# Last group's sums stored by POOL's own queue, and the weight rows for the sums loaded from the fifth step on

## The chip, the core and the metric

The kernel runs on one core of a Trainium2 chip. TensorE (PE) multiplies, VectorE (DVE), ScalarE (ACT) and GpSimd (POOL) work element by element, and SyncE (SP) issues most of the transfers between the chip's main memory and the on-chip buffer. Each engine works its own list of instructions in the order in which they stand; an instruction that waits holds up all behind it on that engine or queue. The metric is the time of the whole program on the device, in microseconds: 1392.29 us before, the median of 3 runs (1391.9 to 1397.92).

## The reference

One encoder layer on 1024 tokens of width 1024: a mixer (mLSTM and neighbourhood attention), then an MLP, then a gated embedding. The change lies in the MLP's second half:

```
z = einsum('bsd,df->bsf', rms_norm(h, norm2_g), w_ff1)        # 1024 x 4096
h = h + einsum('bsf,fd->bsd', square(relu(z)), w_ff2)         # back to 1024 x 1024
gate = sigmoid(einsum('bsd,de->bse', rms_norm(h, ple_norm_g), w_ple_gate))
h = h + gate * einsum('bsk,kd->bsd', p, w_ple_up)
```

## The kernel before

Everything is computed transposed (features on partitions, tokens along the free axis). Every float32 operand of a product is split into a rounded high half and a low half, `hi` by ACT and `lo = raw - hi` by DVE, and each product is three passes on PE: hi x hi, hi x lo, lo x hi (`passes`). Big products are done by Strassen-Winograd: both operands are cut into 2 x 2 blocks, and seven products of sums of blocks replace eight.

**First half of the MLP (`ff1`).** A loop over 16 groups c of 256 of the 4096 inner features. `products` makes a group's blocks in `z{c}_0` and `z{c}_1`; `finish(c)` (L1286) scales and clips them on DVE (L1290), squares them on ACT (L1291), and makes the sums of blocks that Winograd needs next, four POOL operations: `t3`, `t2` into the tile `tz` (L1302, L1303), then two in place in the z tiles (L1306, L1308). All blocks and sums are stored to the scratch tensors `zd[0]` to `zd[3]` in main memory: `put` (L1296) sends three through ACT's queue and the four that POOL made through `PQ`, which is SP's queue.

**Second half (`ff2`).** Four sweeps, `ff2_sweep` (L1377), in the order 2, 0, 1, 3. A sweep walks the 16 groups in steps c = 0 to 15 and adds 24 matmuls a step into eight PSUM banks (L1390, tile `f_P`). A step needs its two operands, each in halves: from `zd[i]` the tile `zr` is loaded (L1276) and split into `zh` (ACT, L1277) and `zl` (DVE, L1278); from w_ff2 the tile `w2r` is loaded in two pieces (L1235) and split into `w_Nh` (ACT, L138) and `w_Nl` (DVE, L141; N is the step). The operands of steps 0, 1 and 2 of the first sweep are asked for while the last group of the first half is still worked on (`ff2_early`); those of the later steps follow by `step(i, c)`. `zr`, `zh`, `zl`, `w_Nh` and `w_Nl` have two buffers each, `w2r` has three: so `w2r` of step c+3 is loaded when `w_Nl` of step c is done, and `w_Nh` of step c+2 can be made when PE has done step c.

**The sums of weight rows.** Sweeps 0 and 1 need Winograd sums of blocks of w_ff2. `w2_load(c)` loads two full row blocks, `w2re` (even) and `w2ro` (odd), 512 KB each; `w2_sums(c)` makes four DVE operations of 128 x 512 of them (L1250 to L1253). `w2re` has six buffers, `w2ro` two, so the third `w2ro` waits for the first pair's sums. During the first sweep the table `ahead` tells after which step which load or sum is asked for; five pairs are summed there, the rest in sweep 0.

The program's text sets which buffers and dependencies there are; a scheduler then puts the instructions in order on every engine and queue, so a moved line shifts its neighbours too. Each transfer that SP or ACT issues takes one of eight completion counters in turn and waits until the transfer eight before it has landed.

Of the kernel before, what the change touches and what calls it, by code (L numbers as in the profile page):

```python
# [59 lines left out]
def tile_block(ctx, tc, xT, pT, w_in, w_out, w_ff1, w_ff2, w_gate, w_up, vecs, gate_b, rpbp, con,  # L60
               outT, dbg=None):
    nc = tc.nc
# [18 lines left out]
    def utile32(name):  # L81
        return big.tile([P, T], F32, tag="u", bufs=16, name=name)
# [33 lines left out]
    zd = [dr.tile([P, FF // 256, T], F32, name=f"zd{i}") for i in range(3)]  # L116
# [1066 lines left out]
    NC_ = FF // 256  # L1183
# [6 lines left out]
    with tc.tile_pool(name="ff1", bufs=1) as ff1:  # L1190
# [37 lines left out]
        PQ = nc.sync  # L1228
# [57 lines left out]
        def finish(c):  # L1286

            z = zt.pop(c)
            for z_ in z:
                V.scalar_tensor_tensor(z_, z_, 0.0, Rb, op0=ALU.max, op1=ALU.mult)  # L1290
                S.activation(z_, z_, AF.Square)  # L1291
            b11, b12, b21, b22 = z[0][:, 0:512], z[0][:, 512:], z[1][:, 0:512], z[1][:, 512:]
            tz = utile32(f"tz{c}")
            t3, t2 = tz[:, 0:512], tz[:, 512:]

            def put(i, s, src):  # L1296
                (PQ if (i, s) in ((0, 1), (1, 1), (1, 0), (3, 0)) else nc.scalar).dma_start(zd[i][:, c, s * 512 : (s + 1) * 512], src)

            put(2, 1, b11)
            put(2, 0, b21)  # L1300
            put(0, 0, b22)
            G.tensor_tensor(t3, b22, b12, op=ALU.subtract)  # L1302
            G.tensor_tensor(t2, t3, b11, op=ALU.add)  # L1303
            put(0, 1, t2)
            put(1, 1, t3)
            G.tensor_tensor(b12, b12, b11, op=ALU.subtract)  # L1306
            put(1, 0, b12)
            G.tensor_tensor(b21, b21, t2, op=ALU.subtract)  # L1308
            put(3, 0, b21)
# [49 lines left out]
    with tc.tile_pool(name="ff2", bufs=2) as ff2:  # L1359
# [108 lines left out]
            E_.tensor_tensor(hres[e][:, cs], hres[e][:, cs], z, op=ALU.add)  # L1468
            nc.sync.dma_start(outT[e * P : (e + 1) * P, cs], hres[e][:, cs])

        ahead = {4 + 2 * c: [(w2_sums, c), (w2_load, c + 2)][: 2 if c < 4 else 1] for c in range(5)}
        ahead[2] = [(w2_load, 0), (w2_load, 1)]
        op, _ = ff2_sweep(2, 0, ("P2", "P1"), pre, ahead, 0)
        op, _ = ff2_sweep(0, 1, ("P3", "P6"), op, {}, 1)
        early3, u_tile = [], utile
# [114 lines left out]
```

## Time and profile before

| what | us |
|---|---|
| median of 3 runs | 1392.29 |
| the profiled execution's own time | 1395.88 |
| its span, first to last instruction | 1394.1 |
| PE busy | 1320.1 (95%) |
| DVE busy | 904.5 (65%) |
| ACT busy | 590.4 (42%) |
| POOL busy | 491.2 (35%) |

The first half of the MLP ends at about 982 us of the span; the first sweep of the second half runs to about 1079 us, the last to about 1299 us, the gate to the end. Shares of the whole span tell little here: PE is nearly always busy, and what counts is where it is not. A step of a sweep is 24 matmuls; a wait of PE at a step shows in the list of waits as PE at `f_P L1390` waiting for a half `w_Nh` or `w_Nl` of that step. The mean granted clock of TensorE over the span is 0.964.

### The profile page before, as it was taken

To read this page: it belongs to the slowest core of one execution; us is meant where nothing else is said; L and a number is where in the kernel's file an instruction comes from. 1 tells how busy PE (TensorE), PEld (TensorE's weight loads), DVE (VectorE), ACT (ScalarE), POOL (GpSimd) and SP (SyncE) were. 2 spreads that over 40 slices of the span, in tenths; PEclk is the share of its full clock that TensorE was granted. 3 is DMA by queue.
4 is the path that set the end of the run, shared out by engine and by line. 5 is a ranking of instruction groups with operands and counts; after the bars stand their busy time and mean duration, and the time that the engine had idled before them with its cause. 6 is when DMAs were issued, how large, how long until landed. Compare 5 with 4: busy or idle time off the path is not lost.

```text
span 1394.1 us, 19257 instructions
## 1 busy us (share of the span) xinstructions
PE 1320.1 (95%) x7115; PEld 1106.7 (79%) x7115; DVE 904.5 (65%) x1435; ACT 590.4 (42%) x955; POOL 491.2 (35%) x392
## 2 busy tenths in 40 slices
PE   7999999999998899997899999999799999999998
PEld 5988778799897677775678888888588888888887
DVE  4486786665672555669856666666565987559543
ACT  7353434264553545545333333333333434545321
POOL 2215675463331111106355556665300000007422
PEclk9999999999998798998899999999899999999999
DMA  8553333475322553311154444554787863542342
GB/s 295 195 151 90 112 111 107 150 249 167 112 62 98 167 168 135 112 46 45 31 166 145 149 136 151 166 166 144 255 307 242 263 199 99 171 145 70 106 143 83
DMA packets 153422, 206.03 MB, mean 148 GB/s; under 512 B 17776, under 2 KB 102768, under 8 KB 153328
## 3 DMA queue, kind: packets, MB, share of 16 engines
q1 hardware_dynamic: 144656, 185.77, 41.6%
q10 hardware_dynamic: 7200, 13.11, 2.8%
q0 software_dynamic: 1472, 5.92, 1.2%
q8 instruction: 56, 0.92, 0.3%
q14 instruction: 38, 0.31, 0.1%
HBM read 151.60 MB, written 53.17 MB: 147 GB/s over the span
## 4 chain that ended last, share of the span: by engine, by line
PE 61%; DMA 5%; DVE 4%; issue 2%; ACT 1%; POOL 1%; SPq 0%; DVEq 0%; ACTq 0%; POOLq 0%
PE f_P L1390 21%; PE p_s_t L256 9%; PE g L1459 6%; PE p L256 6%; PE op L1023 4%; PE p_s L256 3%; PE p_t L256 3%; DMA tab<-tabI 2%; PE pv L995 1%; PE pt L975 1%; PE o1p L310 1%; DMA nr<-qnd 1%; DVE h L1025 1%; DMA wo_0r<-w_out 1%; PE sc L945 1%
## 5 line engine op out<-in xcount | busy, mean ns | idle before, releaser
L1413 POOL TENSOR_TENSOR h<-h,evP 128x512 f32<-128x512 f32 x8 | 14.8, 1886 | 249.2 <-ACT evP L1404 249.2
L256 PE MATMUL p<-b,w_ah 128*128 128x512 f32 x256 | 80.4, 396 | 3.4 <-DVE b L193 3.4
L1278 DVE TENSOR_TENSOR zl<-zr,zh 128x1024 fp32r<-128x1024 f32 x56 | 69.1, 1237 | 11.0 <-ACT zh L1277 11.0
L964 POOL TENSOR_SCALAR pc<-pc,st 128x288 f32<-128x288 f32 (+1 forms) x32 | 17.5, 546 | 159.1 <-DVE st L959 128.9
L1277 ACT ACTIVATE zh<-zr 128x1024 fp32r<-128x1024 f32 x56 | 58.5, 1049 | 23.7 <-DMA zr<-zd 12.2
L260 DVE TENSOR_TENSOR z<-z,p_s_t 128x512 f32<-128x512 f32 x64 | 42.5, 685 | 33.4 <-PE p_s_t L256 32.1
L256 PEld LDWEIGHTS p<-b,w_ah 128*128 128x128 f32 x256 | 49.0, 192 | 14.1 <-DVE b L193 3.9
L954 ACT ACTIVATE pc<-pc,st 128x288 f32<-128x288 f32 (+1 forms) x64 | 36.3, 568 | 53.6 <-DVE st L953 53.5
L256 PE MATMUL p<-b,w_al 128*128 128x512 f32 x128 | 50.9, 399 | 7.7 <-DVE w_al L141 7.7
L1302 POOL TENSOR_TENSOR tz<-z,z 128x512 f32<-128x512 f32 x16 | 26.2, 1639 | 81.0 <-ACT z L1291 81.0
L953 DVE CUSTOM_DVE_ANT_1 pc<-sc,tab 128x288 f32<-128x288 f32 (+1 forms) x64 | 29.8, 503 | 38.2 <-DMA tab<-tabU 16.8
L1459 PE MATMUL g<-gh,wg_h 128*128 128x512 f32 (+1 forms) x136 | 51.6, 380 | 0.0
L1459 PE MATMUL g<-gh,wg_l 128*128 128x512 f32 (+1 forms) x136 | 51.3, 377 | 0.0
L1459 PE MATMUL g<-gl,wg_h 128*128 128x512 f32 (+1 forms) x136 | 51.2, 377 | 0.0
L788 POOL TENSOR_SCALAR wv<-vh,wj 128x129 f32<-128x129 f32 x56 | 30.7, 551 | 57.4 <-PE num L789 52.8
L1290 DVE SCALAR_TENSOR_TENSOR z<-z,Rb 128x1024 f32<-128x1024 f32 x32 | 50.2, 1573 | 0.9 <-ACT Rb L180 0.9
L138 ACT ACTIVATE w_bh<-w_0r 128x1024 fp32r<-128x1024 f32 x16 | 17.0, 1061 | 73.0 <-POOL w_0r L234 53.3
L138 ACT ACTIVATE w_ah<-w_0r 128x1024 fp32r<-128x1024 f32 x16 | 17.0, 1062 | 68.4 <-PE p_t L256 68.4
L256 PE MATMUL p_s_t<-bt,w_bh 128*128 128x512 f32 x128 | 41.9, 410 | 3.4 <-ACT w_bh L138 3.4
L1291 ACT ACTIVATE z<-z 128x1024 f32<-128x1024 f32 x32 | 33.9, 1060 | 22.1 <-DVE z L1290 21.8
L141 DVE TENSOR_TENSOR w_cl<-w_1r,w_ch 128x1024 fp32r<-128x1024 f32 x16 | 23.1, 1443 | 29.2 <-ACT w_ch L138 29.0
L256 PE MATMUL p_s<-b,w_bh 128*128 128x512 f32 x128 | 40.0, 394 | 0.0
(719 smaller groups left out, 4602.5 us busy)
## 6 DMA issues: line engine op xcount, KB each, us to landing
zr<-zd SPq DMA_DIRECT2D x56, 512.0 KB
zd<-z ACTq DMA_DIRECT2D x48, 256.0 KB
w2r<-w_ff SPq DMA_DIRECT2D x48, 256.0 KB
w_0r<-w_ff SPq DMA_DIRECT2D x16, 512.0 KB
w_1r<-w_ff SPq DMA_DIRECT2D x16, 512.0 KB
zd<-tz SPq DMA_DIRECT2D x32, 256.0 KB
zd<-z SPq DMA_DIRECT2D x32, 256.0 KB
w2re<-w_ff SPq DMA_DIRECT2D x16, 512.0 KB
```

Of the source, the lines that this page charges most:

```text
L138: mark["hi"] = S.activation(hi, raw, AF.Copy).ins
L256: TE.matmul(ps, x_, y_, start=j == 0 and i == 0, stop=j == 3 and i == 2)
L260: mark["add"] = V.tensor_tensor(o, a, b, op=ALU.add).ins
L788: G.tensor_scalar(wv, vh[:, c, 0:129], wj[:, col], 1.0, op0=ALU.mult, op1=ALU.mult)
L954: S.activation(pb, pb, AF.Exp, scale=-1.0, bias=st[:, 0:1], accum_out=st[:, 1:2])
L1023: TE.matmul(ps, a, b, start=n == 0 and i == 0, stop=n == len(ks) - 1 and i == 2)
L1277: S.activation(hi, raw, AF.Copy)
L1278: dv.append(V.tensor_tensor(lo, raw, hi.bitcast(F32), op=ALU.subtract).ins)
L1290: V.scalar_tensor_tensor(z_, z_, 0.0, Rb, op0=ALU.max, op1=ALU.mult)
L1291: S.activation(z_, z_, AF.Square)
L1390: pe_last = TE.matmul(ps[n, e], a, b, start=st and k == 0, stop=sp and k == 2)
L1459: TE.matmul(ps, x_, y_, start=k == 0 and i == 0, stop=k == KT - 1 and i == 2)
```

## The change

`finish` of the last group (c = 15) sends the four stores of POOL's sums through POOL's own queue; those of the other 15 groups stay on SP's. The table `ahead` loads the first two pairs after step 5 instead of after step 2, and asks for the sums, each with the load of a later pair, after steps 6, 8, 10, 12, 14 instead of 4, 6, 8, 10, 12.

```diff
             def put(i, s, src):
-                (PQ if (i, s) in ((0, 1), (1, 1), (1, 0), (3, 0)) else nc.scalar).dma_start(zd[i][:, c, s * 512 : (s + 1) * 512], src)
+                ((nc.gpsimd if c == NC_ - 1 else PQ) if (i, s) in ((0, 1), (1, 1), (1, 0), (3, 0)) else nc.scalar).dma_start(zd[i][:, c, s * 512 : (s + 1) * 512], src)
...
-        ahead = {4 + 2 * c: [(w2_sums, c), (w2_load, c + 2)][: 2 if c < 4 else 1] for c in range(5)}
-        ahead[2] = [(w2_load, 0), (w2_load, 1)]
+        ahead = {6 + 2 * c: [(w2_sums, c), (w2_load, c + 2)][: 2 if c < 4 else 1] for c in range(5)}
+        ahead[5] = [(w2_load, 0), (w2_load, 1)]
```

SP's queue before, from the load of `zr` for step 2 of the first sweep on (in these names `zr2_3` is sweep 2, step 3; `w2re_0` is the even row block of pair 0; a last number is the buffer's; `zd1`, `zd0`, `zd3` are the scratch tensors that the sums of group 15 go to):

```order
L1276 DMA zr2_2_9101<-zd2_108 128x1024
L1235 DMA w2ro_0_9216<-w_ff2 128x1024
L1235 DMA w2re_1_9218<-w_ff2 128x1024
L1235 DMA w2ro_1_9220<-w_ff2 128x1024
L1276 DMA zr2_3_9222<-zd2_108 128x1024
L1297 DMA zd1_107<-tz15_9118 128x512
L1297 DMA zd0_106<-tz15_9118 128x512
L1297 DMA zd1_107<-z15_0_8974 128x512
L1235 DMA w2r2_3_9228<-w_ff2 128x512
L1297 DMA zd3_109<-z15_1_8975 128x512
L1235 DMA w2r2_3_9228<-w_ff2 128x512
```

SP's queue now, at the same place:

```order
L1276 DMA zr2_3_9214<-zd2_108 128x1024
L1276 DMA zr2_2_9101<-zd2_108 128x1024
L1235 DMA w2r2_3_9220<-w_ff2 128x512 x2
L1276 DMA zr2_4_9251<-zd2_108 128x1024
L1235 DMA w2r2_4_9257<-w_ff2 128x512 x2
L1235 DMA w2re_0_9325<-w_ff2 128x1024
L1235 DMA w2r2_5_9294<-w_ff2 128x512
L1276 DMA zr2_5_9288<-zd2_108 128x1024
L1235 DMA w2r2_5_9294<-w_ff2 128x512
L1235 DMA w2ro_0_9327<-w_ff2 128x1024
L1235 DMA w2re_1_9329<-w_ff2 128x1024
L1235 DMA w2ro_1_9331<-w_ff2 128x1024
```

The four stores are gone from SP's queue, the loads for step 3 stand where the first pairs' loads stood, and the pairs stand behind the loads for steps 3 to 5. The next loads are `zr2_6`, `w2r2_6` (two pieces), `w2re_2`, `w2ro_2`, `w2r2_7`.

The four stores on POOL now, between the operations that make what they store:

```order
L1302 TENSOR_TENSOR tz15_9118<-z15_1_8975,z15_0_8974 128x512
L1303 TENSOR_TENSOR tz15_9118<-tz15_9118,z15_0_8974 128x512
L1297 DMA zd1_107<-tz15_9118 128x512
L1297 DMA zd0_106<-tz15_9118 128x512
L1306 TENSOR_TENSOR z15_0_8974<-z15_0_8974 128x512
L1297 DMA zd1_107<-z15_0_8974 128x512
L1308 TENSOR_TENSOR z15_1_8975<-z15_1_8975,tz15_9118 128x512
L1297 DMA zd3_109<-z15_1_8975 128x512
```

Before, the four operations stood here alone.

DVE now, from the low half `zl` of step 3 on (`w2_2_3l` is the weights' low half of sweep 2, step 3; `sk0` holds two of the sums of pair 0):

```order
L1278 TENSOR_TENSOR zl2_3_9216<-zr2_3_9214,zh2_3_9215 128x1024
L1251 TENSOR_TENSOR sk0_9370<-w2re_0_9325 128x512
L1278 TENSOR_TENSOR zl2_4_9253<-zr2_4_9251,zh2_4_9252 128x1024
L141 TENSOR_TENSOR w2_2_3l_9224<-w2r2_3_9220,w2_2_3h_9223 128x1024
L1250 TENSOR_TENSOR sk0_9370<-w2re_0_9325,w2ro_0_9327 128x512
L1252 TENSOR_TENSOR w2re_0_9325<-sk0_9370,w2re_0_9325 128x512
L1253 TENSOR_TENSOR w2re_0_9325<-w2ro_0_9327,w2re_0_9325 128x512
L1251 TENSOR_TENSOR sk1_9453<-w2re_1_9329 128x512
L141 TENSOR_TENSOR w2_2_4l_9261<-w2r2_4_9257,w2_2_4h_9260 128x1024
L1250 TENSOR_TENSOR sk1_9453<-w2re_1_9329,w2ro_1_9331 128x512
L1252 TENSOR_TENSOR w2re_1_9329<-sk1_9453,w2re_1_9329 128x512
L1253 TENSOR_TENSOR w2re_1_9329<-w2ro_1_9331,w2re_1_9329 128x512
```

Before, all eight sums of pairs 0 and 1 stood ahead of the weights' low half of step 3; now one stands ahead of it and four more ahead of that of step 4. After these rows come the low halves of step 5, the four sums of pair 2, and only then the low halves of step 6.

## Rows read from the trace of the kernel before

**Rows 1.** Windows: busy us (instructions) per engine, granted clock, DMA share, GB/s

```profile
1000.00:1050.00 50.00, 41.23 (x175) 33.93 (x175) 25.84 (x28) 16.48 (x17) 2.50 (x3) 0.90 0.86 298
```

**Rows 2.** The waits from 960 to 1100 us: who, for whom, total, times, longest

```profile
ACT w_3h L138 <- DMA w2r<-w_ff: 14.3, 1, 14.3
...
PE f_P L1390 <- ACT w_3h L138: 8.8, 1, 8.8
```

**Rows 3.** The chain of waits: start, length, what ran or moved

```profile
991.57 6.78 POOL tz L1302
...
1002.89 4.66 DMA w2r<-w_ff
...
1008.85 290.33 PE f_P L1390 x1272
```

**Rows 4.** PE's timeline around the wait: start, length, operation

```profile
999.70 0.39 PE L1390 MATMUL f_P<-zh,w_2l 128*128 128x512 f32 x1
1008.85 0.77 PE L1390 MATMUL f_P<-zh,w_3h 128*128 128x512 f32 x1 [8.77 <-ACT w_3h L138]
...
1012.71 0.40 PE L1390 MATMUL f_P<-zh,w_3h 128*128 128x512 f32 x1
```

**Rows 5.** SP's queue over the same stretch

```profile
982.70 0.46 SPq L1276 DMA_DIRECT2D zr<-zd  x1
998.38 2.02 SPq L1297 DMA_DIRECT2D zd<-tz  x2
...
1001.71 0.38 SPq L1235 DMA_DIRECT2D w2r<-w_ff  x1
...
1024.13 0.33 SPq L1276 DMA_DIRECT2D zr<-zd  x1
1024.50 0.91 SPq L1235 DMA_DIRECT2D w2r<-w_ff  x2
1025.45 0.43 SPq L1235 DMA_DIRECT2D w2re<-w_ff  x1
```

**Rows 6.** DVE's timeline: in brackets the idle time before and what ended it

```profile
982.63 1.22 DVE L141 TENSOR_TENSOR w_0l<-w2r,w_0h 128x1024 fp32r<-128x1024 f32 x1
...
986.10 1.22 DVE L141 TENSOR_TENSOR w_1l<-w2r,w_1h 128x1024 fp32r<-128x1024 f32 x1
...
990.64 1.21 DVE L141 TENSOR_TENSOR w_2l<-w2r,w_2h 128x1024 fp32r<-128x1024 f32 x1
...
997.24 1.67 DVE L1253 TENSOR_TENSOR w2re<-w2ro,w2re 128x512 f32<-128x512 f32 x1
...
1031.33 0.69 DVE L1251 TENSOR_TENSOR sk<-w2re 128x512 f32<-128x512 f32 x1 [0.65 <-DMA w2re<-w_ff]
```

**Rows 7.** ACT's timeline before step 2, brackets as in the last group

```profile
985.86 1.07 ACT L1277 ACTIVATE zh<-zr 128x1024 fp32r<-128x1024 f32 x1 [1.34 <-DMA zr<-zd]
988.48 1.06 ACT L1291 ACTIVATE z<-z 128x1024 f32<-128x1024 f32 x1 [1.55 <-DVE z L1290]
```

**Rows 8.** The windows view of short stretches, for DMA share and GB/s

```profile
984.00:989.00 5.00, 5.00 (x22) 4.13 (x23) 5.00 (x6) 2.11 (x3) 0.00 (x0) 1.00 1.03 415
1000.00:1005.00 5.00, 0.09 (x1) 0.00 (x0) 0.00 (x0) 0.00 (x0) 2.50 (x3) 0.73 0.65 216
...
1010.00:1045.00 35.00, 35.00 (x151) 28.80 (x150) 22.69 (x25) 13.23 (x14) 0.00 (x0) 0.96 0.87 309
...
975.00:980.00 5.00, 5.00 (x24) 4.14 (x23) 0.69 (x1) 0.20 (x1) 0.79 (x1) 1.00 0.98 295
1008.80:1012.70 3.90, 3.85 (x9) 3.07 (x10) 2.39 (x3) 2.11 (x2) 0.00 (x0) 0.52 1.02 387
```

**Rows 9.** POOL's operation L1302, all 16 of it: ns min/median/max

```profile
L1302 POOL TENSOR_TENSOR tz<-z,z x16: 1286/1298/6781, 705.6 to 991.6; 128x512 f32<-128x512 f32 x16
```

**Rows 10.** Transfers that POOL issued early in the program

```profile
L421 POOL DMA_DIRECT2D upd<-up x8: 531/556/766, 13.5 to 37.9; - x8
...
DMA to landing us min/median/max: 3.4/7.4/12.0
```

## The prediction

> **What bounds the kernel now.** I read the windows first, since PE is busy for 95% of the span and an average hides where it is not. In the stretch from 1000 to 1050 us PE works 41.2 of 50 us [rows 1]: about 9 us are lost there. The list of waits names it: PE waits 8.8 us, once, for `w_3h`, the weights' high half of step 3 of the first sweep, and ACT waits 14.3 us for the transfer of `w2r` that it makes it from [rows 2]. The chain of waits tells why that transfer is late. It runs through POOL's first subtraction of the last group (6.78 us), then to the second piece of `w2r`, issued at 1002.89 and landed after 4.66 us, and from 1008.85 on it is PE alone for 290 us [rows 3]. SP's queue shows the link: it issues the load of `zr` of step 3 at 982.70, then nothing until 998.38, where the stores of POOL's sums begin, and the first piece of `w2r` at 1001.71 [rows 5]. In between SP stands at a store whose data POOL has not made, with the loads of step 3 behind it. They could have gone earlier: their buffer is free when `w_0l` is done, 982.63 + 1.22 = 983.9 [rows 6].
>
> **The stall that goes.** Three parts of the change meet here: the four stores leave SP's queue, the pair loads step behind those of steps 3 to 5, and of the eight sums on DVE ahead of the low half of step 3 one is left. The last matmul of step 2 starts at 999.70, the next at 1008.85, with 8.77 us idle before it [rows 4]. That is the first term, -8.8 us. The second is the clock: after 8.8 us of idling the granted clock is 0.52 of full speed from 1008.8 to 1012.7 [rows 8], the lower of its two levels, 1.2 GHz, and 9 matmuls take 1012.71 - 1008.85 = 3.86 us [rows 4, 8]. At the later pace of 290.33 us for 1272, 0.228 us each [rows 3], they would take 2.05. So -1.8 us, if PE does not pause. Together -10.6 us.
>
> Is step 3 then ready at 999.9? Now `w2r` of step 3 can be issued from 983.9, `w2r` of step 4 from 987.3, when `w_1l` is done, and `w2re` of pair 0 about 0.9 us after that, at 988.2. A `w2re` issued at 1025.45 had landed when DVE took it at 1031.33 [rows 5, 6], so 5.9 us; pair 0's is there by 994.1. DVE then does one sum (0.69), `zl` of step 4 and `w_3l` (1.2 each), done near 997.3. PE wants `w_3l` with its third matmul, at 1000.4: 3 us to spare. ACT now makes `zh` of step 3 ahead of that of step 2, 1.07 us more; hidden, as ACT has `zh` of step 2 done at 986.9 and next waits for DVE until 988.48 [rows 7].
>
> **What is late next: the pairs.** The bytes that used to arrive during the stall must now arrive while PE works, and the sums stand on DVE ahead of the splits that PE needs. The tightest place is step 6. A step is 24 x 0.228 = 5.45 us, so step 6 should start at 999.9 + 3 x 5.45 = 1016.3. Behind the third `w2ro` DVE has four sums (4 x 0.69) and the two low halves of step 6 (2 x 1.22), 5.2 us, and PE wants the last of them 0.2 us into the step: that `w2ro` must have landed by 1011.3. Ahead of and with it go, from 983.9 on, 8 pieces of `w2r` and 7 stores (0.262 MB each) and 3 `zr` and 6 row blocks (0.524 MB each): 3.93 + 4.72 = 8.65 MB. The rate has rows on both sides: 415 GB/s in 984 to 989 where only large blocks move, 295 with stores among them, and 309 over the 35 us from 1010 to 1045, the same mix as here, with the DMA engines 87% busy [rows 8]. These give 20.8, 29.3 and 28.0 us. Landing after the last byte costs about 1.5 us: the `w2re` of 1025.45 took 5.9 us, and the 1.57 MB issued with it since 1024.13 [rows 5] 4.4 at 309/0.87 = 355 GB/s. A gap of about 1.5 us is mine, an estimate: `w2r` of step 5 may not go before 991.9, when `w_2l` is done [rows 6], and the third `w2ro` waits for the first pair's sums. At 355 GB/s (24.4 us) the block lands at 1011.3, just in time; at 309, 3.6 us late; at 295, 4.9 late; at 415 early. So this term lies between 0 and about 5, and I take +2.0, between the 355 and the 309 of the row that is nearest. Later steps have less: a pair every second step makes 1.57 MB per 5.45 us, 289 GB/s, under the 309 that was kept up.
>
> The Trainium skill (page "DMA: Bandwidth & Descriptors", section "Specifications") puts the main memory's limit for one core at about 358 GB/s; the 415 of a 5 us stretch lies above it, so here it is no cap. By it the block would land 24.2 us after 983.9, gaps apart, and the term would be 0 instead of 2.
>
> **The stores on POOL.** Four issues of 0.53 to 0.77 us, landing in 3.4 to 12.0 us for twice the bytes [rows 10]. POOL has no other work until the last sweep, and what it stored is read, and its tiles are taken again, from sweep 0 on, which begins some 75 us later. Cost 0; without that cover it would be the 2.2 us of issue. POOL's operations disturb DVE, though: the subtraction that takes 1.30 us in the median took 6.78 under an unbroken run of DVE work [rows 9], and DVE's sum beside POOL's next one took 1.67 instead of 0.69 [rows 6]. Four such would cost DVE up to 4 x 1.0 us between 992 and 1002, where `w_3l` has 3 us to spare: 0 to 1 us, and I take 0.
>
> The Trainium skill (page "SBUF — State Buffer", section "SBUF: two separate sides") says that of a DVE operation with two on-chip inputs and a POOL operation that reads there, the second is shut out until the first ends. The 6.78 us agree with it. By the rule each of the four POOL operations (1.3 us) could hold DVE for its whole length, 5.2 us in all, 2 beyond the spare, and the sum would be 2 us smaller.
>
> **The sum.** Against the profiled execution's own 1395.88 us: -8.8 - 1.8 + 2.0 = -8.6, so 1387.3. That execution is 3.6 us above the median of the three runs; taken from the median, 1392.3 - 8.6 = 1383.7 us.
>
> **The rivals.**
> - The pairs give back most of it. If the rate under load is that with stores, 295 GB/s, step 6 loses 4.9 us, and steps 7 to 9, which have DVE's sums ahead of their splits too, some more: 3.6 to 10 us given back, net 0.6 to 7, about 1388. For it: DVE already waited 0.65 us for a pair's transfer at 1031 [rows 6] when pairs came slower than they will. Against it: PE waited for nothing in the 290 us after 1008.85 [rows 3], with DMA at 309 GB/s on average.
> - Slower. The same transfers, so slow that step 6 loses over 10.6 us. The third `w2ro` would have to land after 1011.3 + 10.6 = 1021.9; less the 3 us for gap and landing that is 35 us for 8.65 MB, 247 GB/s. Below that rate the change loses. At the 216 GB/s of 1000 to 1005 [rows 8] it takes 40 us, and the time is 1392.3 + 5 = 1397. Against it: in that window the queue stood still between stores, at a DMA share of 0.65.
> - The stall stays. Another wait holds the loads of step 3, say `zr` of step 3, which must wait until PE has left the first half's buffers, or ACT stops at a store of its own behind `w2r`. Then 1392 as before. Before, `zr` of step 3 was issued at 982.70 behind three such loads [rows 5], so this needs a wait that the trace does not show.
> - More than the sum: no give-back and the stall's own cost higher than in this execution, 1381 or less.
>
> **How the numbers follow.** Forecast, a give-back of 0 to 3.6 us: 0.60, 1381.7 to 1385.3, with 1383.7 taken. Most given back: 0.23. Slower: 0.07. Stall stays: 0.04. More than the sum: 0.06. A change of 0.5%, 7.0 us, is about what a measurement of this kernel tells from none. Faster by more: the forecast and the last, 0.66. Within it: most given back and stall stays, 0.27. Slower: 0.07. The range of 8 in 10 takes the forecast and most of the second case, 1381 to 1390; the likeliest case's own is 1381.7 to 1385.3.
>
> **What would show it.** Right: PE's wait for `w_3h` gone from the list, the granted clock at 1.0 from 1000 to 1015, four stores on POOL's queue, `w2r` of step 3 issued near 984; any new wait of PE is at steps 6 to 9, for low halves, with DVE waiting for `w2ro` or `w2re` in front, 0 to 4 us in all. Wrong: PE still idle at step 3 (then it was not the stores), over 5 us idle at steps 6 to 9 (the rate is mis-sized), or a wait in sweep 0 for what POOL stored.

## The result: 0.5% faster, and the profile after

The changed kernel takes 1386.82 us (median of 7 runs: six of 1380.4 to 1389.56, and one disturbed run of 6101.51, which the ratio leaves out), the kernel before 1392.29 (median of 7 runs beside them). The ratio is 0.9946, with a 95% interval of 0.9922 to 0.997; the two medians alone give 0.996. The forecast was 1383.7, in a range of 1381 to 1390, and faster by over 0.5% as the likeliest outcome; the interval does not tell 0.5% from a little less.

The profiled execution has a span of 1386.2 us. The windows of the stretches that [rows 1, 8] showed before (PE, PEld, DVE, ACT, POOL busy, granted clock, DMA share, GB/s):

```profile
1000.00:1050.00 50.00, 49.18 (x218) 40.35 (x217) 35.36 (x38) 17.14 (x17) 2.28 (x3) 1.00 0.91 326
995.00:1015.00 20.00, 19.18 (x85) 15.53 (x84) 16.43 (x16) 5.69 (x7) 6.88 (x8) 1.00 1.02 378
1010.00:1045.00 35.00, 35.00 (x157) 28.96 (x156) 24.32 (x27) 12.09 (x13) 0.00 (x0) 1.00 0.92 324
```

PE works 49.2 of the 50 us in which it worked 41.2, and the clock is full throughout. PE's waits from 960 to 1100 us are now these three:

```profile
PE f_P L1390 <- DVE w_0l L141: 1.2, 1, 1.2
PE f_P L1390 <- DVE w_3l L141: 0.8, 1, 0.8
PE f_P L1390 <- ACT w_0h L138: 0.5, 1, 0.5
```

The first and the last are those of step 0, which the kernel before has too. The 8.8 us for `w_3h` [rows 2] are gone; 0.8 us for the low half `w_3l` of the same step are new. The chain of waits shows where they come from:

```profile
984.17 1.23 DVE w_0l L141
...
985.45 5.30 PE f_P L1390 x22
...
997.53 3.07 DVE zl L1278
1000.59 2.24 DVE w_3l L141
1002.88 288.20 PE f_P L1390 x1270
1291.08 5.44 PE g L1459 x24
```

The chain no longer runs through POOL's subtraction and the late transfer [rows 3], but through two low halves on DVE that took 3.07 and 2.24 us. On SP's queue none of POOL's four stores stands in front of the loads of step 3; they are issued as soon as `w_0l` is done (compare [rows 5]):

```profile
985.42 1.21 SPq L1235 DMA_DIRECT2D w2r<-w_ff  x2
986.68 0.42 SPq L1276 DMA_DIRECT2D zr<-zd  x1
988.88 0.80 SPq L1235 DMA_DIRECT2D w2r<-w_ff  x2
989.73 0.43 SPq L1235 DMA_DIRECT2D w2re<-w_ff  x1
```

**How to compare two profiles here.** Single runs of one kernel scatter by some 10 us, so I measure the stretch that the change touches: from the first product of the second half to the gate's first product, called the sweeps below. It went from 1299.19 - 981.86 = 317.33 us to 1291.08 - 983.40 = 307.68, which is 9.65 less. Ahead of it the changed kernel was 1.54 us later, in code that the change does not touch; behind it both take 95 us to the end of the span. So -9.65 + 1.54 + 0.2 gives the 7.9 us between the two spans.

### The profile page after: what moved, and what is told of

It reads as the page before. It is cut to its first block, busy times and chain, and to the rows that moved or that the text cites. A ratio compares the mean times of both kernels' runs of the same rounds, so it can differ in the third digit from the quotient of the medians.

```text
span 1386.2 us, 19262 instructions
## 1 busy us (share of the span) xinstructions
PE 1315.0 (95%) x7115; PEld 1102.3 (80%) x7115; DVE 913.4 (66%) x1435; ACT 590.7 (43%) x955; POOL 487.4 (35%) x396
## 4 chain that ended last, share of the span: by engine, by line
PE 61%; DVE 5%; DMA 5%; issue 2%; ACT 1%; SPq 0%; POOL 0%; DVEq 0%; POOLq 0%; ACTq 0%
PE f_P L1390 21%; PE p_s_t L256 9%; PE g L1459 6%; PE p L256 6%; PE op L1023 4%; PE p_s L256 3%; PE p_t L256 3%; DMA nr<-qnd 2%; PE pv L995 1%; PE pt L975 1%; PE o1p L310 1%; DMA tab<-tabI 1%; DVE h L1025 1%; PE sc L945 1%; PE nb L841 1%
## 5 line engine op out<-in xcount | busy, mean ns | idle before, releaser
L953 DVE CUSTOM_DVE_ANT_1 pc<-sc,tab 128x288 f32<-128x288 f32 (+1 forms) x64 | 29.9, 503 | 41.2 <-DMA tab<-tabU 21.0
L1302 POOL TENSOR_TENSOR tz<-z,z 128x512 f32<-128x512 f32 x16 | 22.0, 1375 | 81.1 <-ACT z L1291 81.1
```

## The experiments

All sweeps are taken from one profile each. The third column has PE's waits in them as the list of waits shows them, without those of step 0, which all kernels have. The fourth is what the sweeps take beyond the 306.55 us of the last kernel, which has no other wait.

| kernel | sweeps, us | PE's new waits, step: us | beyond 306.55, us | median, us | ratio to before, 95% |
|---|---|---|---|---|---|
| before | 317.33 | 3: 8.77 | 10.78 | 1392.29 | |
| before, second profile | 317.43 | 3: 8.60 | 10.88 | 1393.75 (one run) | |
| changed | 307.68 | 3: 0.82 | 1.13 | 1386.82 | 0.9946 [0.9922, 0.997] |
| changed, again | 309.24 | 3: 0.81; 9: 0.66 | 2.69 | 1384.86 | 0.9929 [0.9908, 0.9949] |
| changed, third | 307.69 | 3: 0.81 | 1.14 | 1385.06 | 0.9946 [0.9925, 0.9967] |
| stores alone | 308.81 | 5: 0.36; 8: 1.05 | 2.26 | 1385.25 | 0.9948 [0.9926, 0.997] |
| loads alone | 312.17 | 5: 3.37 | 5.62 | 1386.76 | 0.9955 [0.9938, 0.9972] |
| two groups' stores | 309.66 | 3: 0.71; 9: 1.81 | 3.11 | 1384.88 | 0.9934 [0.9912, 0.9957] |
| sums on DVE | 310.12 | 9: 1.24 | 3.57 | 1384.75 | 0.995 [0.9928, 0.9972] |
| wait filled | 315.70 | 5: 0.21 | 9.15 | 1391.83 (one run) | |
| more bytes | 309.47 | 5: 1.27; 8: 1.05 | 2.92 | 1382.85 (one run) | |
| sums behind low halves | 306.55 | none | 0 | 1383.32 | 0.9939 [0.9916, 0.9961] |

The intervals of the timed kernels overlap, so medians do not tell them apart; the profiles do.

**What a wait costs.** The idle time in the list is less than its price, as the starts of steps 3, 4 and 5 in the changed kernel show:

```profile
1001.45 0.39 PE L1390 MATMUL f_P<-zh,w_3h 128*128 128x512 f32 x1
...
1008.04 0.39 PE L1390 MATMUL f_P<-zh,w_4h 128*128 128x512 f32 x1
...
1013.48 0.39 PE L1390 MATMUL f_P<-zh,w_5h 128*128 128x512 f32 x1
```

Step 4 takes 5.44 us, as every step does whose operands are ready. Step 3 takes 6.59, 1.15 more, where the list has 0.82: the first products behind the wait start further apart (0.34 us and twice 0.24 instead of 0.23). A short wait is not listed at all. So the price of a wait is read from the fourth column, or from a step's length against 5.44. (Of the 9.15 us of the filled wait, 8.6 are the products that fill it.)

**The two kernels again.** The kernel before, for a second profile:

> The kernel before itself, for a second profile. Theory (the sweeps of the kernel before always hold the same wait, and what scatters lies ahead of them in code that the change does not touch): the start of the sweeps lies anywhere from 978 to 986 us, TensorE waits 8 to 9.5 us for the weights' high half of step 3, the clock is at half behind it, and the sweeps take 316.5 to 318 us (317.3 in the first profile). Rival (the wait itself scatters, and the first profile showed a long one, since the medians moved by 5.5 to 8.1 us and the sweeps by 9.65): the wait is 4 to 7 us and the sweeps take 312 to 315.5 us.

The theory holds: sweeps 317.43 us, one wait of 8.60 us at step 3, with the same POOL operation of 6.78 us in front of it and the products of step 3 at half the clock behind it.

```profile
1006.47 0.77 PE L1390 MATMUL f_P<-zh,w_3h 128*128 128x512 f32 x1 [8.60 <-ACT w_3h L138]
```

The changed kernel, in two more comparisons:

> The changed kernel once more, timed beside the others. The four sweeps, from their first matmul to the gate's first, took 317.3 us before and 307.7 after. Theory (the change saves 9.6 us in the sweeps, and what differs elsewhere is scatter of stretches whose code is the same): sweeps 307.7 within 0.5, total 7 to 11 us below before, ratio 0.992 to 0.995. Rival (something before or behind the sweeps got slower by the change, 1.5 us in the first pair of profiles): the start of the sweeps again later than before's 981.9 by 1 us or more, total no more than 8 us below.

> The changed kernel itself, beside the last one on the same chip. Theory: the sweeps take 307.5 to 309.5 us, with 0.8 us of waiting at step 3 and 0 to 2 us at steps 5 to 9, and the median is 0.5% to 0.7% below that of the kernel before, as in the two comparisons before this (0.9946 and 0.9929). Rival (the 9.65 us of the first profile were a lucky draw): the sweeps take over 311 us.

Sweeps of 309.24 and 307.69 us, 8.1 to 9.75 us less than before over all profiles. The first of them misses the expected 307.7 within 0.5: steps 4, 7 and 9 took 0.28, 0.35 and 0.95 us longer than 5.44 there, and only the last shows in the list. The start of the sweeps lay at 981.9 and 979.6 us before, at 983.4, 978.5 and 980.9 in the changed kernel, so the later start of the first profile did not come again, and this scatter is larger than the difference between the medians (-5.5, -8.1 and -6.4 us; the means, without the disturbed run, differ by -7.5, -8.9 and -8.0) and the sweeps. (The filled wait, below, leaves a second possibility open.)

**The two parts of the change alone.** First only the stores, with the old table of loads (the cuts are against the changed kernel):

```diff
-        ahead = {6 + 2 * c: ...}
-        ahead[5] = [(w2_load, 0), (w2_load, 1)]
+        ahead = {4 + 2 * c: ...}
+        ahead[2] = [(w2_load, 0), (w2_load, 1)]
```

> Only the stores of the last group go to POOL's queue; the pair loads and sums stay where they were. Theory (one wait did it: SP at a store; without it the loads of step 3 go at about 984 and the sums on DVE end in time): PE's 8.8 us wait gone, sweeps 307 to 309 us, as fast as the whole change. Rival (both parts are needed, since seven of the eight sums stand on DVE ahead of the low half of step 3): PE waits 2 to 6 us for w_3l, sweeps 310 to 315.

No wait at step 3, sweeps 308.81 us, between the 307.68 and 309.24 of the whole change. The stores' place in SP's queue was the cause of the wait; taking them out does it alone, and no run shows a gain from moving the loads as well. POOL's first subtraction was held off even longer than before, and nobody waited for it:

```profile
988.10 10.27 POOL L1302 TENSOR_TENSOR tz<-z,z 128x512 f32<-128x512 f32 x1 [15.65 <-ACT z L1291]
```

Then only the loads, with the stores back on SP's queue:

```diff
-                ((nc.gpsimd if c == NC_ - 1 else PQ) if (i, s) in ...
+                (PQ if (i, s) in ...
```

> Only the pair loads and sums move; the four stores stay on SP's queue, where they now stand behind the loads of steps 3 and 4 and the first row block. Theory (one wait did it): step 3 is ready, PE's wait gone, sweeps 307 to 309 us, because SP's stand at the stores ends near 1000 and the loads of step 5 behind them are wanted at 1006.5. Rival (the stand at the stores moves the wait to step 5): PE waits 2 to 6 us at w_5h or w_5l, sweeps 310 to 314.

The wait moved to step 5, as the rival had it, though it is for `zl` and not for the weights: step 3 is served, since its loads now stand in front of the stores, but the first odd row block stands behind them. SP's queue, DVE and PE in this kernel:

```profile
991.82 0.43 SPq L1235 DMA_DIRECT2D w2re<-w_ff  x1
997.80 1.70 SPq L1297 DMA_DIRECT2D zd<-tz  x2
...
1003.10 0.32 SPq L1297 DMA_DIRECT2D zd<-z  x1
1003.48 0.92 SPq L1235 DMA_DIRECT2D w2r<-w_ff  x2
1004.44 0.43 SPq L1235 DMA_DIRECT2D w2ro<-w_ff  x1
```

```profile
1011.51 0.69 DVE L1250 TENSOR_TENSOR sk<-w2re,w2ro 128x512 f32<-128x512 f32 x1 [5.68 <-DMA w2ro<-w_ff]
...
1017.25 1.22 DVE L1278 TENSOR_TENSOR zl<-zr,zh 128x1024 fp32r<-128x1024 f32 x1
```

```profile
1018.52 0.50 PE L1390 MATMUL f_P<-zl,w_5h 128*128 128x512 f32 x1 [3.37 <-DVE zl L1278]
```

SP issues nothing from 992.3 to 997.8, the block comes 5.7 us late for DVE, and `zl` of step 5, behind it on DVE, 3.4 us late for PE. Behind that wait the granted clock was 0.60 from 1018.5 to 1022.7, and step 5 took 5.27 us too long. So the loads alone take 5.2 us off the sweeps and the stores alone 8.5, where both together take 8.1 to 9.75: they do not add.

**More of the same: the stores of group 14 too.**

```diff
-                ((nc.gpsimd if c == NC_ - 1 else PQ) ...
+                ((nc.gpsimd if c >= NC_ - 2 else PQ) ...
```

> As the change, and the stores of the last but one group go to POOL's queue too. In both profiles PE also waits 1.7 us at step 0, for halves made from the load of zr of step 0, which SP issues behind those stores. Theory A: the load goes earlier, that wait shrinks to under 0.5 us, sweeps unchanged from their first matmul on but the span 1.3 to 1.7 us shorter between the first half's last product and step 0's second matmul. Theory B: the load waits for its buffer and not for the stores; nothing changes by more than 0.3 us, and POOL's extra issues (0.6 us each) may hold DVE longer in the last group.

The two waits of step 0 went from 0.5 and 1.2 us to 0.2 and 1.2: hardly anything, and with the stores alone, where group 14's stores are still on SP's queue, they were 0.25 and 1.23 too. So group 14's stores were not what step 0 waits for. The sweeps, 309.66 us, are 0.4 above the slowest of the three profiles of the changed kernel, by a wait at step 9 of the kind that is explained below.

**POOL beside DVE.** In the changed kernel POOL's and DVE's operations around step 3 are these:

```profile
993.11 2.57 POOL L1302 TENSOR_TENSOR tz<-z,z 128x512 f32<-128x512 f32 x1 [15.92 <-ACT z L1291]
995.76 1.29 POOL L1303 TENSOR_TENSOR tz<-tz,z 128x512 f32<-128x512 f32 x1
...
998.20 1.30 POOL L1306 TENSOR_TENSOR z<-z 128x512 f32<-128x512 f32 x1
...
1000.38 1.37 POOL L1308 TENSOR_TENSOR z<-z,tz 128x512 f32<-128x512 f32 x1
```

```profile
996.20 1.41 DVE L1251 TENSOR_TENSOR sk<-w2re 128x512 f32<-128x512 f32 x1 [1.67 <-DMA w2re<-w_ff]
997.53 3.07 DVE L1278 TENSOR_TENSOR zl<-zr,zh 128x1024 fp32r<-128x1024 f32 x1
1000.52 2.31 DVE L141 TENSOR_TENSOR w_3l<-w2r,w_3h 128x1024 fp32r<-128x1024 f32 x1
```

Each DVE operation ends about its own length after the POOL operation beside it: POOL's L1306 ends at 999.50 and `zl`, of 1.22 us elsewhere, at 1000.60; L1308 ends at 1001.75 and `w_3l` at 1002.83; L1303 ends at 997.05 and the sum, of 0.69, at 997.61. Together they take 6.79 us instead of 3.13. Of POOL's first operation it is the other way round: L1302, of 1.30 us, ends 1.14 us after the low half that DVE made until 994.54. To test it, DVE makes the four sums of the last group itself:

```diff
-            G.tensor_tensor(t3, b22, b12, op=ALU.subtract)
+            (V if c == NC_ - 1 else G).tensor_tensor(t3, b22, b12, op=ALU.subtract)
...
-            G.tensor_tensor(b21, b21, t2, op=ALU.subtract)
+            (V if c == NC_ - 1 else G).tensor_tensor(b21, b21, t2, op=ALU.subtract)
```

> The changed kernel with one more edit: the last group's four sums are made by VectorE, ahead of and between the low halves of steps 3 and 4, instead of GpSimd; the four stores stay on GpSimd's queue. Theory (a VectorE operation with on-chip inputs stands still until the GpSimd operation beside it ends): in the changed kernel three VectorE operations between 996 and 1003 us took 1.41, 3.07 and 2.31 us instead of 0.69, 1.22 and 1.22, 3.66 us lost. Now all take 0.69 and 1.22, the four sums cost VectorE 4 x 0.69 = 2.8 us, and the low half of the weights of step 3 stands one low half (1.2 us) earlier, so it is done some 2 us earlier: TensorE's wait of 0.82 us for it is gone, and the sweeps, from the first product of the second half to the gate's first, take 306.5 to 307.5 us (307.7 in the first profile of the changed kernel). Rival (the wait at step 3 comes from what stands in VectorE's queue, not from its neighbour): with 2.8 us more of its own work and 1.2 less in front, the low half comes 1.6 us later, and the wait grows to 2.4 us: 309.3 us. Against the kernel before the median is 0.3% to 0.9% shorter by either, as the start of the sweeps scatters by 3 us.

DVE's rows in this kernel:

```profile
996.35 0.69 DVE L1303 TENSOR_TENSOR tz<-tz,z 128x512 f32<-128x512 f32 x1
...
997.55 0.69 DVE L1251 TENSOR_TENSOR sk<-w2re 128x512 f32<-128x512 f32 x1
...
998.86 1.23 DVE L141 TENSOR_TENSOR w_3l<-w2r,w_3h 128x1024 fp32r<-128x1024 f32 x1
1000.01 1.22 DVE L1278 TENSOR_TENSOR zl<-zr,zh 128x1024 fp32r<-128x1024 f32 x1
```

The theory of the neighbour holds: every operation has its own length, and PE's wait at step 3 is gone although DVE does 2.8 us more. POOL still issues its four stores beside these rows (from 995.59 to 999.92), and with the loads alone, where POOL issues no store, `zl` and `w_3l` took 2.31 us each; so it is POOL's operations, and not its stores, that lengthen them. For the wait itself the run is no clean proof, since `w_3l` also stands one low half earlier in it. The expected 306.5 to 307.5 us are missed, with 310.12, for reasons other than this. Step 9 took 1.56 us too long and step 7 0.39, for sums that stand in front of low halves (the last kernel below; at step 9 DVE stood 4.01 us for the fifth odd row block). And PE waited 0.99 + 1.23 us at step 0 instead of 0.53 + 1.24; behind that the granted clock was 0.57 from 986 to 990, and 21 products took 6.72 us, where 22 took 5.30 in the changed kernel: step 0 was 1.65 us longer.

```profile
985.59 6.72 PE f_P L1390 x21
```

```profile
986.00:990.00 4.00, 4.00 (x12) 3.17 (x11) 4.00 (x5) 2.35 (x3) 0.00 (x0) 0.57 0.84 258
```

**The clock's part of the wait.** The kernel before, with products that add nothing in the place where PE waited:

```diff
+                if i == 2 and c == 2:
+                    for _f in range(38):
+                        TE.matmul(ps[names[0], _f % 4], zfill, zh[:, 0:512], start=False, stop=False)
```

> The kernel before with 38 products more, of a tile of zeros with the high half of step 2, which add zero to the sums: they stand behind step 2 of the first sweep and fill the 8.8 us in which TensorE waited (38 x 0.227 = 8.6 us). Everything else is as before. Theory (the wait cost 1.8 us beyond its own length, because TensorE came back at half its clock): the granted clock stays at 1.0 from 1008 to 1013 us after the wait, the nine products that took 3.86 us take 2.05, and the sweeps take 317.3 - 1.8 = 315.5 us. Rival (the clock's fall was no consequence of the wait, or step 3 is paced by its transfers): the clock is low again or other waits follow, and the sweeps take 317.3 us or more.

The theory holds: the clock stays at 1.00, the products of step 3 follow at 0.23 us, and the sweeps take 315.70 us, 1.6 to 1.7 less than before. The products that fill the wait took 38 x 0.227 = 8.6 us, 0.3 less than the gap of the first profile, and step 5 took 0.55 more. The clock's part is read from step 3 alone: 7.30 us before, 1008.85 [rows 4] to 1016.15, and 7.56 in the second profile, against 5.44 here, so 1.9 to 2.1.

```profile
1016.15 0.39 PE L1390 MATMUL f_P<-zh,w_4h 128*128 128x512 f32 x1
```

```profile
1006.00:1010.00 4.00, 4.00 (x20) 3.30 (x19) 2.90 (x5) 0.00 (x0) 0.00 (x0) 1.00 1.04 401
```

One thing in it was not expected. POOL's first subtraction was not held off here (1.44 us instead of 6.78), and `w_3h` was ready near 1002, some 4 us before the filling products ended at 1006.1. So an execution of the kernel before may have a wait half as long. Its two profiles show 8.77 and 8.60 us; whether the short one comes in it, and how often, was not measured.

```profile
989.24 1.44 POOL L1302 TENSOR_TENSOR tz<-z,z 128x512 f32<-128x512 f32 x1 [15.89 <-ACT z L1291]
990.76 1.61 POOL L1303 TENSOR_TENSOR tz<-tz,z 128x512 f32<-128x512 f32 x1
```

```profile
989.44 1.79 DVE L1250 TENSOR_TENSOR sk<-w2re,w2ro 128x512 f32<-128x512 f32 x1
991.15 1.77 DVE L1251 TENSOR_TENSOR sk<-w2re 128x512 f32<-128x512 f32 x1
```

POOL and DVE take turns here, each waiting for the other.

**The pairs: bytes or order?** Two more transfers, 1.05 MB, behind the odd row blocks of pairs 0 and 1 (stores of step 2's operand to a scratch tensor that nobody reads):

```diff
+            if c < 2: nc.sync.dma_start(extra[c], pre[2][0][c].bitcast(F32))
```

> The changed kernel with two more transfers on SyncE's queue, right behind the odd row blocks of pairs 0 and 1: the halves of the token operand of step 2 are stored to a scratch tensor that nobody reads, 2 x 0.524 MB. Theory (the byte budget of steps 3 to 6 is full, as worked out in the prediction: 8.65 MB had landed just in time): 1.05 MB at 356 GB/s are 2.9 us, so the third odd row block lands some 3 us later against TensorE's place, and TensorE waits 1.5 to 4 us more at steps 5 to 9, for low halves that stand behind sums: the sweeps take 309.5 to 312 us. Rival (the queue has room: the engines of the transfers go faster or the order on VectorE hides it): no more than 1 us beyond the 307.7 to 309.2 of the two profiles of the changed kernel, and waits of VectorE only.

The waits at steps 5 to 9 are 2.3 us in the list and 2.9 in the steps' length, within the theory's 1.5 to 4; the sweeps, 309.47 us, lie just under its 309.5, and only 0.2 above the slowest profile of the changed kernel, which is what the rival allowed, since the wait at step 3 was gone. The scheduler also put DVE's sums in another order, so this run bounds the price of 1.05 MB (0 to 2.9 us) more than it measures it. It is no proof that bytes set the waits.

The last kernel changes only DVE's order: each pair's sums stand behind the low half of the step two before.

```diff
+            with tc.issue_after(dv[-3]) if c < 5 else ExitStack():
-            V.tensor_tensor(s1, a21, a22, op=ALU.add)
+                V.tensor_tensor(s1, a21, a22, op=ALU.add)
...
```

> The changed kernel with one more edit: in the first sweep the four VectorE operations of each pair's sums are ordered behind the low half zl of the step two before, so that pair 0 stands behind zl of step 4, pair 1 behind that of step 6, pair 2 behind that of step 8 and so on, and low halves that TensorE needs sooner stand in front. Theory (the give-back is made in VectorE's queue: a low half waits there behind a sum that waits for its odd row block): TensorE waits nowhere at steps 5 to 9, VectorE may still wait for row blocks, and with one sum less ahead of the weights' low half of step 3 the 0.8 us there shrink below 0.3; the sweeps take 306.5 to 307.3 us (so far 307.7 and 309.2 for the changed kernel). Rival (the give-back is bytes: the operands of steps 5 to 9 themselves land late): waits of 0.5 to 2 us stay at steps 5 to 9, now with w2r or zr ahead of them, and the sweeps take 308 us or more. The median against the changed kernel's moves by less than this measurement tells, 0.1%.

The theory holds to the number: after step 0 PE runs without a wait, and the sweeps take 1286.99 - 980.44 = 306.55 us. Their 56 steps (the fourth sweep has eight, not sixteen) make 304.6 at 5.44 us each, and step 0 takes 1.7 more, as in all these kernels but one.

```profile
982.49 304.50 PE f_P L1390 x1342
1286.99 5.44 PE g L1459 x24
```

POOL still disturbs DVE here, but `w_3l` now stands ahead of the first sum and is done 3 us before PE wants it, so the order alone takes away the wait at step 3:

```profile
994.12 1.92 DVE L141 TENSOR_TENSOR w_3l<-w2r,w_3h 128x1024 fp32r<-128x1024 f32 x1 [0.32 <-ACT w_3h L138]
995.96 2.00 DVE L1251 TENSOR_TENSOR sk<-w2re 128x512 f32<-128x512 f32 x1
```

The same bytes are loaded, so what was given back at steps 4 to 9 came from sums that stood in front of low halves on DVE. In the second profile of the changed kernel this reads:

```profile
1027.50 0.69 DVE L1250 TENSOR_TENSOR sk<-w2re,w2ro 128x512 f32<-128x512 f32 x1 [3.52 <-DMA w2ro<-w_ff]
...
1030.70 1.22 DVE L1278 TENSOR_TENSOR zl<-zr,zh 128x1024 fp32r<-128x1024 f32 x1
```

```profile
1018.97 0.33 SPq L1235 DMA_DIRECT2D w2r<-w_ff  x1
1020.11 0.33 SPq L1276 DMA_DIRECT2D zr<-zd  x1
1020.49 0.42 SPq L1235 DMA_DIRECT2D w2r<-w_ff  x1
1020.97 0.42 SPq L1235 DMA_DIRECT2D w2ro<-w_ff  x1
```

DVE waits 3.5 us for the fifth odd block, which SP issued only at 1020.97, right behind the weights of step 10, which wait for a buffer of their own; its buffer was free at 1012, when the third pair's sums were done. This version has the shortest sweeps here. Its median, 1383.32 us, is below the 1385.06 of the changed kernel on the same chip, but the two intervals overlap; the 1.1 us are shown by the profiles alone, one of this version and three of the changed kernel.

## Why the prediction was right

**The stall, -8.8 us: right.** `w2r` of step 3 was to be issued when `w_0l` is done, near 984; it was issued at 985.42, with `w_0l` done at 985.4, in a profile that is 1.54 us later here. The wait of 8.77 us is gone in every profile of the changed kernel, and the two runs with one half of the change show that it hung on the stores in SP's queue.

**The clock, -1.8: right.** Step 3 took 7.30 and 7.56 us behind the wait and 5.44 with the wait filled, so 1.9 to 2.1. Both terms together were -10.6; the sweeps without any new wait are 10.8 to 10.9 shorter than before.

**The stores on POOL, 0: the mechanism was named, the size was too small.** This is the term that failed. The prediction gave `w_3l` 3 us to spare and allowed POOL to cost DVE four times 1.0 us, then took 0. DVE lost 3.66 us (1.41, 3.07 and 2.31 for 0.69, 1.22 and 1.22), the first even row block came 0.5 us later than worked out, and PE waited 0.82, 0.81 and 0.81 us in three profiles, which made step 3 1.1 us longer. The signs named an idle PE at step 3 as proof against the stores; this one is for `w_3l`, not `w_3h`, and the last kernel removes it with the stores left on POOL. The row of 1.67 us in [rows 6] was taken for the whole of the effect, where it was only the tail of a POOL operation that had started before. The rule of the Trainium skill ("SBUF — State Buffer", section "SBUF: two separate sides") that was weighed there, that one of the two is shut out for the whole instruction, agrees with the three DVE rows; its 2 us were too many, since three of POOL's four operations held DVE up, and in the fourth it was POOL that stood. That the first to start goes first does not agree with all of them: `zl` starts at 997.53, POOL's L1306 at 998.20, and `zl` ends 1.10 us after it. Nor does it give the 6.78 us, in which one POOL operation stood while eight of DVE's started and ended, one after the other.

**The pairs, +2.0: too much, and at the wrong step.** Step 6 was not late in the changed kernel. Its third `w2ro` was to have landed by 1011.3; shifted by the 1.54 us of the start and the 1.1 us at step 3 that is 1013.9, and DVE took it at 1013.42. So it was just in time, as the forecast had it for 355 GB/s; the core moved 378 GB/s from 995 to 1015, not the 309 of the nearest row (the Trainium skill, "DMA: Bandwidth & Descriptors", section "Specifications", has a limit of about 358 for the main memory, by which the term was 0: the term agrees in two profiles of three, the limit itself was passed over 20 us). That row was a stretch whose loads came as buffers fell free, DMA share 0.87 [rows 8]; with loads queued the share was 1.02. (The 1.5 us that the working has for landing are no clean reading: it takes 4.4 us, counted from 1024.13, off 5.9 counted from 1025.45. From one start it would be 2.8, and the block 1.3 us late.) What was given back, 0, 1.6 and 0 us in three profiles, came at steps 4, 7 and 9, most of it at step 9, which the prediction had set aside by comparing average rates (289 below 309 GB/s). An average says nothing of one block that is issued late because of what stands in front of it in SP's queue.

**The sum.** In the sweeps -10.8 for stall and clock, +1.1 for step 3 and 0 to 1.6 for the pairs make -9.7 to -8.1; measured, -8.1 to -9.75. The forecast was -8.6: the two wrong terms, +2.0 for 0 to 1.6 and 0 for 1.1, nearly cancel, and that the total came so near is luck in this part. The median of 1386.82 is 3.1 us above the forecast, and two later ones, 1384.86 and 1385.06, are 1.2 and 1.4 above. The medians fell by 5.5 to 8.1 us and the means by 7.5 to 8.9, the sweeps by 8.1 to 9.75; with intervals of some 3 us to either side these agree, and if anything is lacking it is either the scatter ahead of the sweeps or executions of the kernel before with a shorter wait; which of the two, the runs do not settle.

**The rivals.** Most given back: no, 1.1 to 2.7 us of 10.8. Slower: no; the rate over the whole stretch, 984 to 1013, was 346 GB/s, not 247. The stall stays: no; but with the loads alone a wait of 3.4 us does come back at step 5. More than the sum: no. A wait in sweep 0 for what POOL stored: none.

## What to carry to other kernels

A store that waits for its data holds every load behind it on the same queue: look for the gap in the queue's timeline, and count which of the two remedies (move the store, or move the urgent loads in front) leaves nothing behind it. Before an operation is given DVE or POOL work beside it, take its time as that of both, one after the other. When one wait goes, look for the next in the order of the neighbouring engine's list, as here: put what the busy engine needs in front of what only waits for memory.

## What the runs showed of the hardware that was not expected

- Of DVE and POOL, both working on two on-chip inputs, one stood still while the other worked. POOL's subtraction of 1.30 us took 6.78 [rows 9] and even 10.27 us under an unbroken run of DVE operations, and got its turn only near that run's end. With the wait filled the two alternated: four DVE sums in a row took 1.77 to 1.79 us instead of 0.69, and POOL's four 1.44 to 1.74. In both cases POOL started 0.2 us ahead of the same DVE sum, and in the changed kernel a `zl` that started 0.67 us ahead of POOL's L1306 was the one that stood; so the order of the starts does not tell which of the two goes first, and what does is open.
- The granted clock fell to 0.57 (from 986 to 990, sums on DVE) behind waits of 0.99 and 1.23 us at step 0, and stayed at 1.00 behind 0.53 and 1.24 (changed) and behind 0.73 and 1.24 (loads alone).
- POOL's stores took 0.5 to 0.6 us each to issue and landed 6.4 to 8.1 us later in the changed kernel; nothing waited for them.
- The start of the sweeps lay between 976.6 and 985.5 us in kernels that differ little in their text up to there. Where that scatter arises was not studied.
